# Heads transposed a tile later, averages paired, the last tile's banks in another order: one change to the front of an encoder layer

## The chip, the cores and the metric

One core of a Trainium2 chip runs the whole program. The metric is the time of one execution on the device, in microseconds (us); with several runs, their median. The core has four engines that compute: TensorE (PE; its weight load is listed as PEld), VectorE (DVE), ScalarE (ACT) and GpSimd (POOL). SyncE (SP) issues most of the DMA transfers, POOL a few. The engines run side by side, each its own instructions in a fixed order, and wait for each other by semaphores. TensorE writes into PSUM banks; ACT and DVE take the results from there.

## What is computed

One layer of an encoder over 2048 tokens of width 1024: attention of 8 heads with forget gates beside a pooling over trailing windows of 2, 4, 8 and 16 frames, then cross attention to 256 memory tokens, then SwiGLU. Cut to what the change touches:

```python
def rmsnorm(x, g):
    return x * lax.rsqrt(jnp.mean(x * x, axis=-1, keepdims=True) + EPS) * g
...
xn = rmsnorm(h, g_mix[l])
z = jnp.einsum('bsd,dc->bsc', xn, w_in[l])          # q, k, v, p_in, f_logit side by side
q = rmsnorm(head_split(q, FOX_HEADS, FOX_HEAD_DIM), g_q_fox[l]).transpose(0, 2, 1, 3)
k = rmsnorm(head_split(k, FOX_HEADS, FOX_HEAD_DIM), g_k_fox[l]).transpose(0, 2, 1, 3)
c = jnp.cumsum(jax.nn.log_sigmoid(f_logit), axis=-1)
s = q @ k * scale + c[t] - c[s]; causal softmax; fox = p @ v
mixed = trailing mean of p_in over POOL_WINDOWS[g] frames - p_in, group g of 4
pool = (mixed @ w_pool[g]) * pool_scale
h = h + concat(fox, pool) @ w_out[l]
mn = rmsnorm(mem, g_mem_kv[l]); mkv = mn @ w_mem_kv[l]   # 256 memory tokens
...
h = h + cross attention of h to mkv (4 heads)
h = h + SwiGLU(rmsnorm(h, g_ffn[l]))
```

All matmuls of the projections are made in three products (high by high, low by high, high by low parts of float32), so each "matmul" below stands for three instructions.

## The kernel before

**Stage A** (0 to about 102 us) computes the 512 pooling columns, transposed, in eight blocks of 256 tokens, while the weights of the other 1544 columns arrive and are split (`split_w_in`). For the norms it needs sums of squares of each token row: `load_rows(i)` fetches the 128 tokens of tile i (two loads), `square_rows(i)` squares them on ACT with a running sum, and `row_stats(T)` turns four tiles' sums into the factors `rstd` and stores them.

**The tile loop** (about 102 to 416 us) runs over 16 tiles of 128 tokens, i = 2b + j. `project(i, j, hs, ls, banks)` makes 1544 columns in four PSUM banks of 386, 24 matmuls each; there are four such buffers, so bank n of a tile can start when bank n of the tile before has been copied out. `scaled` does that on ACT, times `rstd`, into a slab z. `normed_heads` then splits v into high and low parts and stores it, adds the gates' bias, and takes the squares of q and k with their sums (DVE) and their inverse roots (POOL). One tile later `split_heads` multiplies q and k by these and by the gains (DVE), and splits the result: a cast on ACT, the low part on DVE (`kl`, L55). `to_heads` transposes it: 16 transposes on PE in four groups q = 0 to 3 (L410), each copied to a stage buffer `st` by ACT (L412) and stored by SP (L413) in `qkT`. Before, groups 0 to 2 stand at the end of the tile in which `split_heads` was run, right behind that tile's last bank, and group 3 behind bank 0 of the next.

In the same loop run the 16 pooled averages, w = 4T + g for token quarter T and window group g. `window_load` fetches the columns; `window` (DVE) multiplies by `rstd` (rows `rb`), makes g + 1 additions of shifted columns (L204), subtracts the frame (L459) and splits (L199 on ACT, L55 on DVE); `pooled` (PE) applies the group's map in the single PSUM bank `ss`, and its second half copies it out (ACT, L478) and stores it in `poolT` (POOL, L479). Before, one average stands in each of tiles 0 to 5 and 8 to 13, and two in tiles 6 and 7. The loop also prepares the output weights (`out_sums`) in eight of the tiles.

These steps take their buffers from 14 job slots `jl`. A freed slot goes to the end of a list and the next request takes the first of the list, so the order of frees in the program decides which earlier use a new one waits for, its store included. `in_order` fixes the order of DVE, ACT, POOL and SP as the program has it.

**The memory stage** (about 416 to 460 us) makes the keys and values of the memory, `kv(0)` to `kv(15)`, each six matmuls in three products of a weight block that `split_kv(n)` has split (ACT L194, DVE L195). Among them stand tile 15's `split_heads` and `to_heads`, the matmuls of the memory's squares `ssp`, and `cumulated`, which makes the running sum of the gates in steps, one at each `next(cum)`: two DVE steps (L519, L520), log and exponent on ACT (L521, L522, with a table load), a difference on DVE (L524), totals by a matmul with ones (L527), sums inside the blocks by a triangular matrix (L533), a transpose (L537), a store in `cd`. SP issues the 16 weight loads `kr`, then head 0's queries and keys of the first three token quarters (15 loads), then the last four stores. Then **head 0** starts (scores `sps`, L799), and the rest of the program follows to 2594 us.

Of the kernel before, what the change touches and what calls it, by code (L numbers as in the profile page):

```python
# [8 lines left out]
F32 = mybir.dt.float32  # L9
# [7 lines left out]
P = 128  # L17
# [23 lines left out]
def block_kernel(ctx: ExitStack, tc: tile.TileContext, x, xT, memT, cols, rows, w_qkvf, w_p, w_pool, w_out,  # L41
# [128 lines left out]
    def x_split(tiles, part=None, qs=range(4)):  # L170

        for q in qs:
            n, raw = tiles[q]
            hi = xp.tile([P, 2, B], F32R, tag="xhi", name="xhi", bufs=8)
            act.copy(hi[:], raw[:])
            if part is not None:
                sq = part.v if q == 0 else zp.tile([P, 4, P], F32, tag="st", name="sq", bufs=4)[:].rearrange("p a c -> p (a c)")
                act.activation(sq.rearrange("p (a t) -> p a t", a=2), raw[:], AF.Square, scale=1.0 / 32.0)
                if q:
                    pool.tensor_tensor(out=part.v, in0=part.v, in1=sq, op=ALU.add)  # L180
# [54 lines left out]
    head0, zs_home = [], hpa  # L235
    with xstack, in_order(EN.DVE, EN.Activation, EN.Pool, EN.SP):
        was = ExitStack()
        wa = opened(was, "wa", side="right")
# [49 lines left out]
        msx = small([P, NT], "msx")  # L288
        rows_in = {}

        def load_rows(i):
# [46 lines left out]
        for b in range(1, NB):  # L338
            hs, ls = x_parts(xt)
            nxt_raw = x_load((b + 1) % NB)  # L340
            load_w_in(b)
            for s_ in stores:
                s_()
            zs = [zpp.tile([P, 2, B], F32, tag="z", name="zp", bufs=4) for _ in range(2)]
            load_rows(b - 1)
# [5 lines left out]
            square_rows(b - 1)  # L351
# [16 lines left out]
        def scaled(i, zps):  # L368
            z = slab(i % 2)
            for n in zps:  # L370
                act.activation(z[:, n * ZB:(n + 1) * ZB], zps[n][:], AF.Copy, scale=rstd[:, i:i + 1])
            return z

        def normed_heads(i, z):

            vq = slab(3)
# [4 lines left out]
            sp.dma_start(vd[:, :, i, :].rearrange("h p c -> p h c"), vq[:, :1024].rearrange("p (h c) -> p h c", h=H))  # L381
            dve.tensor_tensor(out=fl[:, :, i], in0=z[:, 1536:1544], in1=bfor, op=ALU.add)

            qn = vq[:, 1024:]
# [3 lines left out]
            dve.tensor_reduce(out=ms[:], in_=qf, axis=AX.X, op=ALU.add)  # L388
            rq = small([P, 2 * H], "zrq", 2)
            rsqrt(rq[:], ms[:])  # L390
            return z, qn, rq

# [11 lines left out]

        def to_heads(i, zr, qs):
            for q in qs:
# [5 lines left out]
                act.copy(st[:], tp[:])  # L412
                sp.dma_start(qkT[q][i // 4][:, :, i % 4 * P:(i % 4 + 1) * P].rearrange("h p t -> p h t"), st[:])  # L413

# [92 lines left out]
        def cumulated():  # L507
# [17 lines left out]
            yield  # L525
            tot = one_bank()
            pe.matmul(tot[:, :HN], lhsT=ones[:], rhs=e, start=True, stop=True)  # L527
# [4 lines left out]
            loc = one_bank()  # L532
            pe.matmul(loc[:, :HN], lhsT=utri, rhs=e, start=True, stop=True)  # L533
            dve.tensor_tensor(out=e, in0=loc[:, :HN], in1=cp[4], op=ALU.add)
# [4 lines left out]
            sp.dma_start(cd[:], mn)  # L539
            yield  # L540

        kvraw, kvw, kvb = {}, {}, {}
        EARLY = 8

# [28 lines left out]
        xt = nxt_raw  # L573
        zr, st_, mxs, jobs = None, None, [], {}
# [3 lines left out]
        pts = {0: window_load(0, 0)}  # L578
        for b in range(NB):
            hs, ls = x_parts(xt)  # L580
            for j in range(2):
                i = 2 * b + j
                if j == 0:
# [3 lines left out]
                if i < 9:  # L587
                    load_rows(i + 7)
                if i >= 12:
                    for n in {14: range(3), 15: range(3, EARLY)}.get(i, ()):  # L590
                        load_kv(n)
                elif i in sums_at:
                    jobs["sums"] = out_sums_load(sums_at.index(i))
# [14 lines left out]
                if i < 9:  # L608
                    square_rows(i + 7)
                if i > 0:  # L610
                    zr = split_heads(*st_)
                if i == NT - 1:
                    split_kv(0)
                    split_kv(1)
                if "sums" in jobs:
                    out_sums(sums_at.index(i), jobs.pop("sums"))
                if i in (0, 4, 8):
                    row_stats((i + 7) // 4)
                if i == NT - 1:
                    was.close()  # L620
                    kvp = opened(xstack, "kvp", side="right")
# [11 lines left out]
        here[0] = kvp  # L633
        jobs_in[0] = Slots(kvp, [P, TB + HIS], "kl", 6)
        kv(0)
        split_kv(2)
        split_kv(3)
        kv(1)
# [5 lines left out]
        mms, mr = small([P, 2], "mms"), small([P, 2], "mr")  # L644
        dve.tensor_copy(mms[:], ssp[:, :2])
        rsqrt(mr[:], mms[:])
        st_ = normed_heads(NT - 1, z)
        for n in range(4, EARLY):
            split_kv(n)
# [6 lines left out]
        cum = cumulated()  # L656
        next(cum)
        next(cum)
        kv(2)
        kv(3)  # L660
        split_kv(8)
        next(cum)
        kv(4)
        zr = split_heads(*st_)
        next(cum)
        kv(5)
        split_kv(9)
        kv(6)
        split_kv(10)
        kv(7)  # L670
        to_heads(NT - 1, zr, range(4))
        next(cum)
        kv(8)
# [4 lines left out]
        for m in range(2):  # L678
            act.activation(msk[m].v, mks[m].v, AF.Square)
        next(cum)  # L680
        load_gates(0, head0[3])
        load_head_part(0, head0, 3)
# [1086 lines left out]
```

## Time and profile before

| | us |
|---|---|
| median of 3 runs | 2598.14 |
| lowest and highest | 2594.37, 2600.2 |
| the profiled execution, its own time | 2595.92 |
| its span in the profile | 2594.1 |
| mean granted TensorE clock | 0.989 |

The profile is one execution. A row of a timeline or a group tells the line of the kernel (L410), the operation, what is written from what, and in brackets how long the engine stood idle before it and what released it. Tile starts in this execution (first matmul of bank 0): tile 1 at 118.57, tile 4 at 176.35, tile 7 at 238.35, tile 8 at 261.74, tile 15 at 397.46; the memory stage starts at 416.47 and head 0 at 460.45.

### The profile page before, as it was taken

To read this page: it belongs to the slowest core of one execution; us is meant where nothing else is said; L and a number is where in the kernel's file an instruction comes from. 1 tells how busy PE (TensorE), PEld (TensorE's weight loads), DVE (VectorE), ACT (ScalarE), POOL (GpSimd) and SP (SyncE) were. 2 spreads that over 40 slices of the span, in tenths; PEclk is the share of its full clock that TensorE was granted. 3 is DMA by queue.
4 is the path that set the end of the run, shared out by engine and by line. 5 is a ranking of instruction groups with operands and counts; after the bars stand their busy time and mean duration, and the time that the engine had idled before them with its cause. 6 is when DMAs were issued, how large, how long until landed. Compare 5 with 4: busy or idle time off the path is not lost.

```text
span 2594.1 us, 37306 instructions
## 1 busy us (share of the span) xinstructions
PE 2519.7 (97%) x12909; PEld 2161.3 (83%) x12909; DVE 1733.9 (67%) x2995; ACT 1297.4 (50%) x2487; POOL 829.0 (32%) x1134
## 2 busy tenths in 40 slices
PE   8999998999999799999999999999999999999998
PEld 8998997788888587788878888888888888888887
DVE  4466564899998755455787778756766666665554
ACT  5455445788889413555643433334543333333443
POOL 0132333445555522344425445431001222222000
PEclk9999998999999999999999999999999999999999
DMA  8775657744542646222554554447773332325765
GB/s 260 218 219 163 186 161 199 208 123 122 150 123 61 191 157 203 89 82 90 179 207 171 195 183 169 168 158 261 244 266 130 104 119 102 122 102 177 233 211 187
DMA packets 248558, 434.01 MB, mean 167 GB/s; under 512 B 30000, under 2 KB 121904, under 8 KB 240688
## 3 DMA queue, kind: packets, MB, share of 16 engines
q1 hardware_dynamic: 215216, 323.59, 39.7%
q0 software_dynamic: 33152, 108.03, 11.4%
q8 instruction: 102, 1.67, 0.3%
q14 instruction: 88, 0.72, 0.1%
HBM read 294.02 MB, written 137.50 MB: 166 GB/s over the span
## 4 chain that ended last, share of the span: by engine, by line
PE 48%; issue 8%; DVE 2%; ACT 1%; DMA 1%; POOL 1%; SPq 0%; POOLq 0%; DVEq 0%; ACTq 0%
PE bk L62 13%; PE bk L60 13%; PE bk L61 13%; PE mmps L60 2%; PE mmps L62 2%; PE mmps L61 2%; PE tp L980 1%; PE obk L60 0%; DVE ww L55 0%; DMA xraw<-hTd 0%; PE obk L62 0%; PE obk L61 0%; POOL out_dram L1662 0%; DMA h<-h1d 0%; ACT mq L1153 0%
## 5 line engine op out<-in xcount | busy, mean ns | idle before, releaser
L55 DVE TENSOR_TENSOR ww<-draw,ww 128x512 fp32r<-128x512 f32 x308 | 204.9, 702 | 156.2 <-ACT ww L199 155.7
L199 ACT CAST ww<-draw 128x512 fp32r<-128x512 f32 x308 | 179.1, 620 | 220.5 <-PE bk L62 175.7
L55 DVE TENSOR_TENSOR ww<-graw,ww 128x512 fp32r<-128x512 f32 x220 | 180.9, 829 | 104.4 <-ACT ww L199 104.0
L61 PE MATMUL bk<-ww,ww 128*128 128x512 f32 x616 | 239.8, 389 | 0.0
L62 PE MATMUL bk<-ww,ww 128*128 128x512 f32 x616 | 239.8, 389 | 0.0
L60 PE MATMUL bk<-ww,ww 128*128 128x512 f32 x616 | 239.8, 389 | 0.0
L199 ACT CAST ww<-graw 128x512 fp32r<-128x512 f32 x220 | 135.8, 621 | 181.8 <-PE bk L62 158.6
L55 DVE TENSOR_TENSOR pl<-tp,ph 128x512 fp32r<-128x512 f32 (+3 forms) x296 | 176.7, 598 | 33.4 <-ACT ph L893 31.6
L812 ACT ACTIVATE s<-s,mx 128x1024 f32<-128x1024 f32 (+2 forms) x192 | 173.7, 905 | 6.0 <-DVE mx L806 5.4
L60 PE MATMUL zps<-wh,xhi 128*128 128x386 f32 x512 | 175.2, 342 | 0.0
L877 PE MATMUL tp<-ident,s 128*128 128x128 f32 x1088 | 172.4, 274 | 2.3 <-DVE pl L55 1.8
L61 PE MATMUL zps<-wl,xhi 128*128 128x386 f32 x512 | 174.1, 340 | 0.0
L62 PE MATMUL zps<-wh,xl 128*128 128x386 f32 x512 | 173.6, 339 | 0.0
L893 ACT CAST ph<-tp 128x512 fp32r<-128x512 f32 (+3 forms) x296 | 148.6, 513 | 41.0 <-PE tp L877 34.7
L877 PEld LDWEIGHTS tp<-ident,s 128*128 128x128 f32 x1088 | 134.5, 142 | 30.9 <-DVE pl L55 5.7
L1662 POOL DMA_DIRECT2D out_dram<-o x32 | 17.3, 540 | 382.6 <-DVE o L1659 381.6
L62 PE MATMUL bk<-qs,ww 128*128 128x512 f32 x352 | 137.3, 390 | 1.4 <-DVE ww L55 1.4
L60 PE MATMUL bk<-qs,ww 128*128 128x512 f32 x352 | 137.9, 392 | 0.3 <-ACT s L1581 0.3
L61 PE MATMUL bk<-kh,ww 128*128 128x512 f32 x352 | 137.0, 389 | 0.0
L60 PE MATMUL bk<-kl,ww 128*128 128x512 f32 x352 | 137.0, 389 | 0.0
L62 PE MATMUL bk<-kl,ww 128*128 128x512 f32 x352 | 137.0, 389 | 0.0
L61 PE MATMUL bk<-cb,ww 128*128 128x512 f32 x352 | 137.0, 389 | 0.0
(608 smaller groups left out, 7275.7 us busy)
## 6 DMA issues: line engine op xcount, KB each, us to landing
graw<-in_w_gu_dram SPq DMA_DIRECT2D x44, 1024.0 KB, 5.4
draw<-in_w_down_dram SPq DMA_DIRECT2D x66, 256.0 KB, 4.4
xl<-in_xT_dram SPq DMA_DIRECT2D x64, 256.0 KB, 4.7
wdr<-in_w_down_dram SPq DMA_DIRECT2D x22, 512.0 KB, 4.6
jl<-in_x_dram SPq DMA_DIRECT2D x32, 256.0 KB, 6.6
vd<-cb SPq DMA_DIRECT2D x16, 512.0 KB, 4.6
cb<-cd SPq DMA_DIRECT2D x8, 1024.0 KB, 7.4
v<-vd SPq DMA_DIRECT2D x8, 1024.0 KB, 5.4
```

The lines of the kernel that those rows point to most:

```text
L55: (eng or dve).tensor_tensor(out=lo, in0=src, in1=f(hi), op=ALU.subtract)
L60: pe.matmul(ps, lhsT=sh, rhs=mh, start=first, stop=False, skip_group_check=goes_on)
L61: pe.matmul(ps, lhsT=sh, rhs=ml, start=False, stop=False, skip_group_check=goes_on)
L62: pe.matmul(ps, lhsT=sl, rhs=mh, start=False, stop=last, skip_group_check=goes_on)
L199: act.copy(hi, raw)
L812: act.activation(s[:, sl], s[:, sl], AF.Exp, bias=ng, scale=-1.0, accum_out=l[:, q, g:g + 1])
L877: pe.transpose(tp[:, q * P:(q + 1) * P], unit["rows"][q][:, j * P:(j + 1) * P], ident[:])
L893: act.copy(ph[:, sl], tp[:, sl])
L980: pe.transpose(tp[:, e_], src[:, q + e_], ident[:])
L1662: pool.dma_start(out[rows_, cs], o)
```

## The change

- `to_heads(i - 2, ...)` now does all four groups in tile i: groups 0 and 1 behind bank 0, groups 2 and 3 behind bank 1. Nothing is transposed at the end of a tile, except tile 13's heads, at the end of tile 14.
- The averages stand in tiles 0 to 11: the short windows (g = 0 and 1) as a pair in tiles 0, 3, 6 and 9, the others one by one.
- Stage A squares ten row groups (before seven), the loop the other six. The output weights are prepared in other tiles.
- The memory's sums of squares are added on DVE (before POOL).
- The last tile makes its banks in the order 3, 2, 1, 0, each copied out at once. `cumulated` stands between them, with the two matmuls of the totals in one bank. The first two weight blocks are split in it. `normed_heads` is cut in `split_v`, `gates` and `norms`.
- Six weight loads are early (before eight), eight come before head 0's loads, two behind them and behind the load of the gates. The memory stage has four job slots of another size and four stage buffers (before six and three).
- The last four stores of heads go out on POOL's queue.

The diff, cut:

```diff
@@ x_split
-                    pool.tensor_tensor(out=part.v, in0=part.v, in1=sq, op=ALU.add)
+                    dve.tensor_tensor(out=part.v, in0=part.v, in1=sq, op=ALU.add)
...
-        stage = lambda name: here[0].tile([P, 4, P], F32, tag="st", name=name, bufs=4 if here[0] is zp else 3)
+        stage = lambda name: here[0].tile([P, 4, P], F32, tag="st", name=name, bufs=4)
...
+        ROWS = (0,), (1, 2), (3, 4), (5, 6), (7,), (8,), (9,)
...
-        row_stats(0)
+        for T in range(2):
+            row_stats(T)
...
-        def to_heads(i, zr, qs):
+        def to_heads(i, zr, qs, queue=sp):
...
-                sp.dma_start(qkT[q][i // 4][:, :, i % 4 * P:(i % 4 + 1) * P].rearrange("h p t -> p h t"), st[:])
+                queue.dma_start(qkT[q][i // 4][:, :, i % 4 * P:(i % 4 + 1) * P].rearrange("h p t -> p h t"), st[:])
...
-            tot = one_bank()
-            pe.matmul(tot[:, :HN], lhsT=ones[:], rhs=e, start=True, stop=True)
-            dve.tensor_copy(cp[3], tot[:, :HN])
+            both = one_bank()
+            tot, loc = both[:, :HN], both[:, HN:2 * HN]
+            pe.matmul(tot, lhsT=ones[:], rhs=e, start=True, stop=True)
+            pe.matmul(loc, lhsT=utri, rhs=e, start=True, stop=True)
+            dve.tensor_copy(cp[3], tot)
...
-        EARLY = 8
+        EARLY = 6
...
-        sums_at = (0, 1, 2, 3, 4, 9, 10, 11)
-        averages = lambda i: [i] if i < 6 else [2 * i - 6, 2 * i - 5] if i < 8 else [i + 2] if i < 14 else []
+        sums_at = (1, 2, 4, 5, 7, 8, 10, 11)
+        AVERAGES = (0, 1), (2,), (3,), (4, 5), (6,), (7,), (8, 9), (10,), (11,), (12, 13), (14,), (15,)
...
-                    to_heads(i - 2, zr, (3,))
+                    to_heads(i - 2, zr, range(2))
...
                     zps.update(project(i, j, hs, ls, range(n, n + 1)))
+                    if n == 1 and i > 1:
+                        to_heads(i - 2, zr, range(2, 4))
...
                 z = scaled(i, zps)
-                if i > 0:
-                    to_heads(i - 1, zr, range(3 if i < NT - 1 else 4))
-                if i < NT - 1:
-                    st_ = normed_heads(i, z)
+                if i == LAST - 1:
+                    to_heads(i - 1, zr, range(4))
+                st_ = normed_heads(i, z)
...
+        next(cum)
+        zps = project(i, 1, hs, ls, (3,))
         ssp = one_bank()
...
+        zr = split_heads(*st_)
+        scaled(i, zps)
...
+        gates(i, z)
         dve.tensor_copy(mms[:], ssp[:, :2])
         rsqrt(mr[:], mms[:])
+        next(cum)
+        zps = project(i, 1, hs, ls, (2,))
+        next(cum)
+        next(cum)
+        scaled(i, zps)
...
+        split_v(i, z, vq)
+        zps = project(i, 1, hs, ls, (1,))
+        to_heads(i - 1, zr, range(4))
+        scaled(i, zps)
...
+        split_kv(0)
+        split_kv(1)
+        zps = project(i, 1, hs, ls, (0,))
+        next(cum)
+        next(cum)
+        scaled(i, zps)
...
+        jobs_in[0] = Slots(kvp, [P, TB], "kl", 4)
         kv(0)
         split_kv(2)
+        st_, rest = norms(z, vq)
         split_kv(3)
+        rest()
         kv(1)
...
-        for n in range(EARLY, 2 * KD):
+        for n in range(EARLY, EARLY + 8):
             load_kv(n)
         head0.extend(load_head(0, hpa, range(3)))
+        load_gates(0, head0[3])
         kv(2)
         kv(3)
+        split_kv(6)
+        kv(4)
+        split_kv(7)
+        for n in range(EARLY + 8, 2 * KD):
+            load_kv(n)
+        zr = split_heads(*st_)
+        kv(5)
...
-        to_heads(NT - 1, zr, range(4))
+        to_heads(LAST, zr, range(4), pool)
```

How the order changes is shown at three places. In the rows, a wait on DMASW is one for a transfer that POOL issued, DMAHW for one of SP's, and the numbers behind a name tell buffers apart.

ACT in tile 4, from a copy of transposed heads (`st`) over the first average's way out of `ss` to the scaled copies of the tile's banks (`zps`). Before:

```order
L412 COPY st<-tp 128x512 [waits DMAHW3_49,PE_49]
L199 CAST jl_2348<-jl_2009 128x512 [waits DVE_49,PE_49]
L478 ACTIVATE jl_2266<-ss,colt 128x512 [waits DMAHW2_49,DMASW3_49,DMAHW6_49,DMASW2_49,DMASW1_49]
L298 ACTIVATE jl_2220,msx_210<-jl_2220 128x512 [waits DMAHW5_49]
L298 ACTIVATE jl_2221,msx_210<-jl_2221 128x512 [waits DMAHW6_49,DMASW6_49]
L401 CAST kl<-cb 128x16x64 [waits DVE_49,Activation_49]
L371 ACTIVATE qs<-zps,rstd 128x386 [waits Pool_49]
L371 ACTIVATE qs<-zps,rstd 128x386 [waits PE_49] x3
```

After (line numbers are those of the changed kernel: L430 is the copy of heads, L496 the average's, L419 the cast of split_heads, L376 the scaled copy):

```order
L430 COPY st<-tp 128x512 [waits DMAHW5_49,PE_49]
L430 COPY st<-tp 128x512 [waits DMAHW6_49,PE_49]
L430 COPY st<-tp 128x512 [waits DMAHW7_49,PE_49]
L430 COPY st<-tp 128x512 [waits DMAHW0_49,PE_49]
L496 ACTIVATE jl_2282<-ss,colt 128x512
L199 CAST jl_2391<-jl_2028 128x512 [waits DMASW4_49,DVE_49,Activation_49]
L496 ACTIVATE jl_2330<-ss,colt 128x512 [waits DMASW7_49,PE_49]
L300 ACTIVATE jl_2228,msx_213<-jl_2228 128x512 [waits DMAHW7_49]
L300 ACTIVATE jl_2229,msx_213<-jl_2229 128x512 [waits DMAHW0_49]
L419 CAST kl<-cb 128x16x64 [waits DVE_49]
L376 ACTIVATE qs<-zps,rstd 128x386 [waits Pool_49]
L376 ACTIVATE qs<-zps,rstd 128x386
```

All four copies of heads now stand ahead of the first average's copy, and a second average's copy behind it; the scaled copies still come last.

DVE in the same tile, the average (L204 multiplies by `rb` and then adds, L459 or L477 is its last step) and the two products of split_heads behind it. Before:

```order
L204 TENSOR_TENSOR jl_2009<-jl_2009,jl_2007 128x512 [waits DMAHW6_49,DMAHW5_49]
L442 COPY jl_2009<-tail_1402 128x16
L444 COPY tail_1402<-jl_2009 128x16 [waits DVE_49]
L204 TENSOR_TENSOR jl_2345<-jl_2009 128x527 [waits DMASW7_49]
L459 SCALAR_TENSOR_TENSOR jl_2009<-jl_2345,jl_2009 128x512 [waits DVE_49]
L55 TENSOR_TENSOR jl_2349<-jl_2009,jl_2348 128x512 [waits Activation_49]
L396 TENSOR_TENSOR cb<-kh,zrq 128x1024 [waits Pool_49]
L398 TENSOR_TENSOR cb<-cb,gqs 128x1024 [waits DVE_49]
L55 TENSOR_TENSOR kl<-cb,kl 128x16x64 [waits Activation_49]
```

After:

```order
L204 TENSOR_TENSOR jl_2028<-jl_2028,jl_1807 128x512 [waits DMAHW2_49]
L460 COPY jl_2028<-tail_1429 128x16
L462 COPY tail_1429<-jl_2028 128x16 [waits DVE_49]
L204 TENSOR_TENSOR jl_2384<-jl_2028 128x527 [waits DMASW2_49,DMASW1_49,DMASW4_49,PE_49,Activation_49]
L204 TENSOR_TENSOR jl_2386<-jl_2384 128x525 [waits DVE_49,PE_49]
L204 TENSOR_TENSOR jl_2388<-jl_2386 128x521 [waits DVE_49]
L477 SCALAR_TENSOR_TENSOR jl_2028<-jl_2388,jl_2028 128x512 [waits DVE_49]
L55 TENSOR_TENSOR jl_2392<-jl_2028,jl_2391 128x512 [waits Activation_49]
L414 TENSOR_TENSOR cb<-kh,zrq 128x1024 [waits Pool_49]
L416 TENSOR_TENSOR cb<-cb,gqs 128x1024 [waits DVE_49]
L55 TENSOR_TENSOR kl<-cb,kl 128x16x64 [waits Activation_49]
```

A window of three additions (w = 6) has taken the place of a window of one (w = 4). Its first addition writes slot `jl_2384`, and waits for DMASW4, which is POOL's store of `jl_2282`, the first average's result in the rows of ACT above.

SP at the end of the memory stage, head 0's loads (`qs`, `kh`, `kl`), the stores of tile 15's heads and of the gates (`cd`), and the gates' load (`cb`). Before:

```order
L219 DMA kh<-qkT2t_94 64x512
L220 DMA kl<-qkT2t_94 64x512
L413 DMA qkT0t_87<-st 128x4x128
L413 DMA qkT1t_91<-st 128x4x128
L413 DMA qkT2t_95<-st 128x4x128
L219 DMA kh<-qkT2t_92 64x512
L413 DMA qkT3t_99<-st 128x4x128
L539 DMA cd<-kl_4678 128x128
L220 DMA kl<-qkT2t_92 64x512
```

After:

```order
L219 DMA kh<-qkT2t_94 64x512
L220 DMA kl<-qkT2t_94 64x512
L223 DMA cb<-cd 128x2048
L569 DMA kr<-in_w_mem_kv_dram 128x512 x2
L216 DMA qs<-qkT0t_87 128x512
L219 DMA kh<-qkT2t_95 64x512
```

The four stores have left SP. The load of the gates has come ahead, and behind it stand the last two weight blocks of the memory, which before were issued ahead of all of head 0's loads.

More of the change, by code (lines that the diff above doesn't have):

```diff
@@ L236, in block_kernel @@
     with xstack, in_order(EN.DVE, EN.Activation, EN.Pool, EN.SP):
+        msmall = opened(xstack, "msmall", side="right")
         was = ExitStack()
@@ L344, in block_kernel @@
             zs = [zpp.tile([P, 2, B], F32, tag="z", name="zp", bufs=4) for _ in range(2)]
-            load_rows(b - 1)
+            for r in ROWS[b - 1]:
+                load_rows(r)
             project_p(hs, ls, zs, range(KD), (0, 1))
@@ L350, in block_kernel @@
             project_p(hs, ls, zs, range(KD), (2, 3))
-            square_rows(b - 1)
+            for r in ROWS[b - 1]:
+                square_rows(r)
             stores.append(keep_p(b, zs, 1))
@@ L381, in normed_heads, with gates, norms @@
             sp.dma_start(vd[:, :, i, :].rearrange("h p c -> p h c"), vq[:, :1024].rearrange("p (h c) -> p h c", h=H))
+        def gates(i, z):
             dve.tensor_tensor(out=fl[:, :, i], in0=z[:, 1536:1544], in1=bfor, op=ALU.add)
+        def norms(z, vq):
             qn = vq[:, 1024:]
@@ L531, in cumulated @@
             yield
-            loc = one_bank()
-            pe.matmul(loc[:, :HN], lhsT=utri, rhs=e, start=True, stop=True)
-            dve.tensor_tensor(out=e, in0=loc[:, :HN], in1=cp[4], op=ALU.add)
+            dve.tensor_tensor(out=e, in0=loc, in1=cp[4], op=ALU.add)
             yield
@@ L586, in block_kernel @@
                     pts[w] = window_load(w % NG, w // NG)
[L587 to L590, printed above, removed]
+                if i < 6:
+                    load_rows(i + 10)
+                if i in sums_at:
+                    jobs["sums"] = out_sums_load(sums_at.index(i))
+                if i >= LAST - 2:
+                    for n in range(3 * (i - LAST + 2), 3 * (i - LAST + 3)):
                         load_kv(n)
-                elif i in sums_at:
-                    jobs["sums"] = out_sums_load(sums_at.index(i))
                 zps = project(i, j, hs, ls, range(1))
                 if i > 1:
-                    to_heads(i - 2, zr, (3,))
+                    to_heads(i - 2, zr, range(2))
                 pos = []
@@ L643, in block_kernel @@
                           stop=c == 1)
-        mms, mr = small([P, 2], "mms"), small([P, 2], "mr")
+        mms, mr = (msmall.tile([P, 2], F32, name=n) for n in ("mms", "mr"))
+        zr = split_heads(*st_)
+        scaled(i, zps)
+        zt[i] = z
+        gates(i, z)
         dve.tensor_copy(mms[:], ssp[:, :2])
         rsqrt(mr[:], mms[:])
-        st_ = normed_heads(NT - 1, z)
-        for n in range(4, EARLY):
-            split_kv(n)
+        next(cum)
[3 more added lines that the diff above has]
+        scaled(i, zps)
+        zt[i] = z
+        split_v(i, z, vq)
+        zps = project(i, 1, hs, ls, (1,))
+        to_heads(i - 1, zr, range(4))
+        scaled(i, zps)
+        zt[i] = z
+        split_kv(0)
[3 more added lines that the diff above has]
+        next(cum)
+        was.close()
+        kvp = opened(xstack, "kvp", side="right")
+        scaled(i, zps)
+        here[0] = kvp
+        jobs_in[0] = Slots(kvp, [P, TB], "kl", 4)
+        kv(0)
+        split_kv(2)
+        st_, rest = norms(z, vq)
+        split_kv(3)
+        rest()
+        kv(1)
+        split_kv(4)
+        split_kv(5)
         lstack.close()
```

67 lines of the change are left out of this document (30 added, 37 removed).

## The prediction

> **What bounds the kernel now.** The page comes first, for the busy shares. Its first part gives each engine's busy time and its share of the span.
>
> ```profile
> span 2594.1 us, 37306 instructions
> PE 2519.7 (97%) x12909; PEld 2161.3 (83%) x12909; DVE 1733.9 (67%) x2995; ACT 1297.4 (50%) x2487; POOL 829.0 (32%) x1134
> ```
>
> TensorE (PE) is busy in 97% of the span, and the change takes no matmul away. All it can gain is time in which PE stands still, or runs at a lowered clock. The second view is the busy time by stretches. I cut it where the loops change: tiles 1 to 5, tiles 6 to 8, tiles 9 to 15, the memory stage (keys and values of the memory), and the start of head 0. The columns are stretch, length, busy time of each engine, granted clock, share of the DMA engines, GB/s.
>
> ```profile
> 130.00:210.00 80.00, 78.76 (x474) 77.17 (x474) 55.31 (x87) 40.84 (x77) 30.33 (x32) 1.00 0.70 206
> 210.00:290.00 80.00, 73.40 (x425) 71.27 (x424) 46.89 (x68) 41.86 (x78) 21.03 (x16) 0.96 0.57 170
> 290.00:416.00 126.00, 125.92 (x766) 124.51 (x764) 76.31 (x101) 59.38 (x102) 41.34 (x34) 1.00 0.57 168
> 416.00:461.00 45.00, 33.25 (x142) 26.14 (x143) 20.91 (x34) 21.23 (x36) 16.57 (x30) 0.81 0.91 245
> 461.00:500.00 39.00, 34.25 (x173) 26.23 (x172) 32.98 (x112) 30.02 (x65) 17.75 (x39) 0.91 0.58 175
> ```
>
> PE loses something at tiles 1 to 8 and much in the memory stage; between 290 and 416 it loses nothing. The third view, the waits of PE from 116 to 500, says what ended the idle time: total, times, longest.
>
> ```profile
> PE tp L410 <- DVE kl L55: 7.8, 7, 2.3
> PE kv L60 <- ACT kw L194: 7.0, 1, 7.0
> PE ss L527 <- DVE kl L524: 4.6, 1, 4.6
> PE sps L799 <- DVE mx L801: 4.2, 4, 2.4
> ```
>
> The first three are what the change touches. The fourth belongs to head 0, whose code stays.
>
> **What the stalls cost, clock included.** PE's timeline after the stall at the end of tile 6:
>
> ```profile
> 236.86 1.69 PE L410 MATMUL tp<-identr,kl 128*128 128x128 f32 x12 [2.29 <-DVE kl L55]
> 239.44 0.53 PE L60 MATMUL zps<-wh,xhi 128*128 128x386 f32 x1
> 240.38 0.34 PE L60 MATMUL zps<-wh,xhi 128*128 128x386 f32 x1
> ```
>
> After 2.29 us of idleness matmuls take 0.53 instead of 0.34 us until 240.4. Against the even pitch of the tile this stretch lost about 1.0 us more than the wait; two of the seven stalls are that long, and the five shorter ones have no such stretch. Wait, issue gaps and slow clock together make **11.3 us** for the seven (7.8 waited, 2.1 of clock, 1.4 of gaps).
>
> In the memory stage, PE's timeline:
>
> ```profile
> 429.20 0.76 PE L527 MATMUL ss<-kl,ones 128*128 128x128 f32 x2 [4.63 <-DVE kl L524]
> 431.04 0.63 PE L60 MATMUL kv<-kw,xhi 128*128 128x512 f32 x1
> 434.88 0.41 PE L60 MATMUL kv<-kw,xhi 128*128 128x512 f32 x1
> 440.45 0.40 PE L60 MATMUL kv<-kw,xhi 128*128 128x512 f32 x1
> 441.15 0.40 PE L60 MATMUL kv<-kw,xhi 128*128 128x512 f32 x1
> 449.74 0.79 PE L60 MATMUL kv<-kw,xhi 128*128 128x512 f32 x1 [7.02 <-ACT kw L194]
> ```
>
> Three matmuls take 0.70 us at 440.45 and 1.28 us at 431.04 (three groups to 434.88). So the wait for the gates, 4.63, cost 2.5 more by the clock, and the wait of 7.02 another 2.9. With 0.9 of small gaps about it the stage loses **18 us**. ACT and SP tell where the 7.02 came from:
>
> ```profile
> 436.79 1.56 ACT L412 COPY st<-tp 128x512 f32<-128x512 f32 x3 [3.02 <-PE tp L410]
> 446.29 0.58 ACT L412 COPY st<-tp 128x512 f32<-128x512 f32 x1 [7.94 <-DMA qkT0t<-st]
> ```
>
> ```profile
> 421.56 4.61 SPq L549 DMA_DIRECT2D kr<-in_w_mem_kv_dram  x8
> 441.13 0.45 SPq L220 DMA_DIRECT2D kl<-qkT2t  x1
> 441.86 0.38 SPq L413 DMA_DIRECT2D qkT0t<-st  x1
> ```
>
> The fourth copy waited for one of three stage buffers; the store that frees it stood in SP's order behind head 0's loads. The weight split that PE needed stood behind this copy on ACT.
>
> **Part 1: heads transposed a tile later.** Transposes and copies stay 16 and 4 a tile. They now read a tile that was split one tile before, so the wait at the tile's end has no cause left: **-11.3**. Late next is the new tile's bank 0, which needs the first scaled copy. That copy stands on ACT behind the cast of split_heads, which stands behind DVE's averages.
>
> **Part 2: pairs of short averages.** The averages' number is the same; the double long ones of tiles 6 and 7 go apart. Rows of tile 0, whose single average becomes two, DVE then ACT:
>
> ```profile
> 110.42 1.08 DVE L204 TENSOR_TENSOR jl<-jl,jl 128x512 f32<-128x512 f32 x1 [3.08 <-DMA jl<-pd]
> 111.63 0.70 DVE L204 TENSOR_TENSOR jl<-jl 128x527 f32<-128x527 f32 x1
> 112.78 0.69 DVE L459 SCALAR_TENSOR_TENSOR jl<-jl,jl 128x512 f32<-128x512 f32 x1
> 114.42 0.69 DVE L55 TENSOR_TENSOR jl<-jl,jl 128x512 fp32r<-128x512 f32 x1 [0.74 <-ACT jl L199]
> ```
>
> ```profile
> 113.77 0.62 ACT L199 CAST jl<-jl 128x512 fp32r<-128x512 f32 x1 [7.15 <-DVE jl L462]
> 114.72 0.63 ACT L298 ACTIVATE jl<-jl 128x512 f32<-128x512 f32 x1 [0.33 <-DMA jl<-in_x_dram]
> 116.04 1.51 ACT L371 ACTIVATE qs<-zps,rstd 128x386 f32<-128x386 f32 x3
> ```
>
> The first average ends on DVE at 115.1. The second adds 1.08, two additions of 0.70, the last step 0.69 and about 0.8 of small copies, so its cast on ACT begins at 119.1; then cast 0.62, two squares 1.32, one scaled copy 0.5: 121.6. PE was to begin tile 1 at 118.6: **+3.0**, and **+1.1** of clock (a wait like the 2.29).
>
> In tiles 4, 7 and 10 PE applies two averages over one PSUM bank. The second waits until ACT has copied the first out, and that copy now stands behind the copies of heads 2 and 3. Rows by group of lines, mean ns after the comma:
>
> ```profile
> L412 ACT COPY st<-tp 128x512 f32<-128x512 f32 x58 | 31.2, 592 | 18.7 <-PE tp L410 18.4
> L401 ACT CAST kl<-cb 128x1024 fp32r<-128x1024 f32 x15 | 15.7, 1046 | 29.6 <-DVE cb L398 29.6
> L478 ACT ACTIVATE jl<-ss,colt 128x512 f32<-128x512 f32 x16 | 11.0, 684 | 0.6 <-PE ss L62 0.6
> ```
>
> From the end of the transposes: about 0.15 until the last copy begins, 0.59 for it, 0.68 for the average: 1.4 each, **+4.2**. It would be nothing if bank 2 stood between; it doesn't.
>
> The same tiles, and tile 1, bring a wait that the diff does not show: the next long average takes a slot that the first average's result has just left, so DVE waits until POOL's store of it has landed. How long that takes is in the view of the tile poolT:
>
> ```profile
> DMA to landing us min/median/max: 2.3/5.9/7.5
> ```
>
> Tile 4, from the start T of its bank 0 (bank 4.38, eight transposes 1.13, first average 0.7): ACT has copied the first average at T+12.9. Landing at 2.3 to 7.5 gives T+15.2 to T+20.4. DVE then needs three additions (2.2), last step and split (2.1 with ACT's cast between), the two products of split_heads (2.4), and ACT the cast of 1.05: 7.9. The first scaled copy ends 0.6 later, at T+23.7 to T+28.9, while PE is through with the tile at T+22.5: a stall of 1.2 to 6.4. I take 2.5 and 1.0 of clock, because at T+13 most of the tile's loads are in. By the same working tiles 1 and 7 give 0.6 each and tile 10 2.1. Together **+6.8** (bounds 1.5 to 17). Short hold-ups behind three more tiles where a pair meets the split of x: **+1.3** (0 to 2).
>
> The tile loop comes out at -11.3 + 4.1 + 4.2 + 6.8 + 1.3 = **+5.1**. Stage A squares ten row groups instead of seven, three times two squares on ACT at 0.8. It has room, by the busy times from 50 to 102:
>
> ```profile
> 50.00:102.00 52.00, 52.00 (x434) 52.00 (x434) 19.46 (x23) 26.68 (x50) 1.48 (x3) 1.00 0.76 247
> ```
>
> PE never stands still there and ACT is idle for 25 us, so these 4.8 us lie beside PE's work: nothing, up to +2 if their 1.5 MB of loads delay weights.
>
> **Part 3: the last tile.** What goes: the 4.63 and 7.02 with their clock, **-18.0** with the gaps. What comes, T0 being PE's end of tile 14:
>
> ```profile
> 403.86 0.69 DVE L55 TENSOR_TENSOR xl<-xl,xhi 128x512 fp32r<-128x512 f32 x1 [0.24 <-ACT xhi L175]
> 405.62 5.77 POOL L180 TENSOR_TENSOR jl<-jl,sq 128x512 f32<-128x512 f32 x3
> ```
>
> - The sums of squares of the memory are matmuls behind bank 3, at T0+5.9 (sixteen transposes 1.67, a bank 4.2). Before, T0 was 396.65 and DVE ended the splits at T0+7.9; three additions, now DVE's at about 0.7 and partly in gaps, end at T0+9.5. Stall 3.7, clock 1.8: **+5.5** (2 to 8).
> - The gates' totals between banks 2 and 1: 0 to the 4.63 of now; bank 2 gives 4.2 of cover. **+1.5**.
> - The last transposes still stand behind norms, split_heads: 2.4 and 1.0 of clock, **+3.4** (0 to 5). One weight split late: **+0.9**.
> - Weights 14 and 15 are now issued behind 15 loads of head 0 and the gates' load. By SP's rows 23 loads took 421.6 to 441.6, so their issue comes at about 443.5 and the landing some 6 later; PE wants them, split, at about 451: **+2.3** (0 to 4.7).
>
> Sum -18.0 + 13.6 = **-4.4**. The last stores no longer wait behind loads; head 0 needs them no sooner than its other loads: nothing.
>
> **Sum.** +5.1 - 4.4 = +0.7 on the profiled execution's 2595.92, 2596.6. That execution lies 2.2 below the median of the runs shown, 2598.14, so in those terms **2598.8**.
>
> **A rule against a row.** The Trainium skill ("TensorE: Matmul & The Clock Gate", part 1, the HAM clock gate) says that the clock falls to half after an idle window of about 3.4 us. By that rule the new stalls under 3.4 us cost no clock, and the sum would be lower by 3.1. The trace disagrees: 2.29 us was enough; I keep the row's price.
>
> **Rivals.**
> - *Landings in time* (20%): the stores land in 2.3 us, weights 14 and 15 arrive early, the squares come without loss of clock: 6.8 + 2.3 + 1.8 less, **2588**. For it: the loads of tile 4 are fewer at T+13 than at its start. Against: the median landing is 5.9.
> - *Only the removed waits count* (10%): 29.3 less and only tile 0's 4.1 added, **2573**. Against it: in tiles 4, 7 and 10 ACT's order alone gives the 1.4.
> - *The slot decides* (20%; the slower side): in tiles 4, 7 and 10 the store lands after 6 to 7.5 us. DVE is late, ACT's cast and the scaled copy behind it, and PE stands at bank 0 of tiles 5, 8 and 11; each adds about 3, with clock, to what I took: **2608**. It decides where the landing takes more than some 4 us.
> - *The wait only changes its name* (8%): DVE's lateness at the ends of tiles 5 to 8 stays and PE waits for the scaled copy in place of the transposes. Half of the 11.3 comes back, less the 1.3 counted: **2603**.
>
> **How the numbers follow.** My forecast has 42%, own range 2593 to 2603. About 0.2%, 5.2 us, is what a measurement of this kernel can tell from no change. Faster: the first two rivals, 0.30. Slower: the third, half the fourth and the upper tail, 0.25. Same: 0.45. The range leaves out the 2573 case and the outer tails: 2584 to 2611.
>
> **What would show it.** Right: no wait of the transposes for kl behind tiles 4 to 8; new waits of the projection for the scaled copy at tiles 1 and 5; of the pooled matmul for ACT in tiles 4, 7, 10; one of the sums of squares for DVE; none for the kw split near 442. Wrong: PE busy through 116 to 416 (then near 2588), or waits of 4 us and more at tiles 5, 8, 11 (then near 2608), or head 0 starting much later than 456 to 460.

## The result and the profile after

The changed kernel is slower: 2621.19 us, the median of 4 runs (2617.75 to 2622.01), against 2596.36 (2594.37 to 2600.2) for the kernel before (4 runs, the three above and one more). The ratio is 1.0091 with a 95% interval of 1.0074 to 1.0109. The profiled execution took 2621.78 against 2595.92.

The first part of the page after, and its waits of PE in the first 520 us, which take in the start of head 0 (engine, line, releaser, total, times, longest). Lines have moved: the copy of heads is L430, the scaled copy L376, the average's way out L496, the score matmul of head 0 L848.

```profile
span 2619.9 us, 37306 instructions
PE 2525.7 (96%) x12909; PEld 2165.7 (83%) x12909; DVE 1733.3 (66%) x2998; ACT 1298.8 (50%) x2487; POOL 820.5 (31%) x1135
```

```profile
PE zps L60 <- ACT qs L376: 12.8, 5, 4.0
PE zps L60 <- ACT kh L376: 8.0, 4, 2.4
...
PE sps L848 <- DVE mx L850: 4.9, 4, 3.1
PE ss L60 <- ACT jl L496: 4.3, 3, 1.4
PE ss L664 <- POOL jl L532: 3.4, 1, 3.4
PE tp L428 <- DVE kl L55: 2.7, 1, 2.7
PE kv L60 <- ACT kw L194: 1.4, 1, 1.4
```

Every wait that the change meant to remove is gone or small: the seven of the transposes in the loop, the 7.02 of the weights' split (1.4 now), the 4.63 of the gates. In their place PE waits nine times for a scaled copy, 20.8 us in all. Before, it did so at no place of the loop. The busy times by stretch, cut as in the prediction, show where: PE stood still for 5.8, 9.8 and 6.1 us, before for 1.2, 6.6 and 0.1. So the loss is spread over the loop, also over its later tiles, which lost nothing before.

```profile
130.00:210.00 80.00, 74.22 (x425) 71.84 (x423) 45.28 (x75) 32.65 (x61) 21.20 (x24) 0.98 0.59 179
210.00:290.00 80.00, 70.17 (x409) 68.43 (x409) 53.77 (x82) 36.50 (x66) 28.37 (x28) 0.98 0.55 165
290.00:416.00 126.00, 119.91 (x724) 118.00 (x723) 67.63 (x90) 56.43 (x95) 32.59 (x30) 1.00 0.56 169
```

**Tile 4 to 5, step by step.** DVE after, in time order:

```profile
190.69 1.07 DVE L204 TENSOR_TENSOR jl<-jl,jl 128x512 f32<-128x512 f32 x1
205.35 2.26 DVE L204 TENSOR_TENSOR jl<-jl 128x527 f32<-128x527 f32 x3 [13.29 <-DMA poolT<-jl]
209.68 1.22 DVE L414 TENSOR_TENSOR cb<-kh,zrq 128x1024 f32<-128x1024 f32 x1
```

ACT and PE over the same stretch:

```profile
198.58 1.07 ACT L430 COPY st<-tp 128x512 f32<-128x512 f32 x2 [4.56 <-PE tp L428]
199.54 0.70 ACT L496 ACTIVATE jl<-ss,colt 128x512 f32<-128x512 f32 x1
212.19 1.04 ACT L419 CAST kl<-cb 128x1024 fp32r<-128x1024 f32 x1 [1.35 <-DVE cb L416]
213.14 2.00 ACT L376 ACTIVATE qs<-zps,rstd 128x386 f32<-128x386 f32 x4
```

```profile
213.77 0.57 PE L60 MATMUL zps<-wh,xhi 128*128 128x386 f32 x1 [4.04 <-ACT qs L376]
```

ACT stood idle for 4.56 us, because its next instruction in order was the copy of the heads' group 2, which PE transposes only behind bank 1. Then came the first average's copy, at 199.5. Its store was issued at 200.53 and landed some 4.8 us later, and that freed the slot for which DVE had waited 13.29 us. The rest is the chain of the prediction: additions, split_heads, cast, scaled copy, PE.

**Tile 3 to 4** shows the same order with another victim. ACT, then DVE, then PE at the start of tile 4:

```profile
175.42 1.07 ACT L430 COPY st<-tp 128x512 f32<-128x512 f32 x2 [4.48 <-PE tp L428]
176.38 0.64 ACT L199 CAST jl<-jl 128x512 fp32r<-128x512 f32 x1
```

```profile
177.04 0.69 DVE L55 TENSOR_TENSOR jl<-jl,jl 128x512 fp32r<-128x512 f32 x1 [2.29 <-ACT jl L199]
```

```profile
186.55 0.65 PE L60 MATMUL zps<-wh,xhi 128*128 128x386 f32 x1 [2.30 <-ACT kh L376]
```

The pair's first average was ready on DVE at 174.8. Its cast stood behind the copies of heads, so DVE lost 2.29 us in the middle of a pair. PE waited 2.30 us for the scaled copy at tile 4's start, and with the slow matmuls behind this wait it lost 4.1. At the pair of tile 6 DVE waited 5.71 us for the same cast, at that of tile 9 2.90.

Head 0 starts at 479.81 against 460.45, 19.4 us later. The other 5 us of the 24.8 between the medians come behind that point.

### The profile page after: what moved, and what is told of

The parts are those of the page before. It is cut to its first block, busy times and chain, and to the rows that moved or that the text cites. A ratio compares the mean times of both kernels' runs of the same rounds, so it can differ in the third digit from the quotient of the medians.

```text
span 2619.9 us, 37306 instructions
## 1 busy us (share of the span) xinstructions
PE 2525.7 (96%) x12909; PEld 2165.7 (83%) x12909; DVE 1733.3 (66%) x2998; ACT 1298.8 (50%) x2487; POOL 820.5 (31%) x1135
## 4 chain that ended last, share of the span: by engine, by line
PE 47%; issue 8%; DVE 2%; ACT 1%; DMA 1%; POOL 1%; SPq 0%; POOLq 0%; DVEq 0%; ACTq 0%
PE bk L62 13%; PE bk L60 13%; PE bk L61 13%; PE mmps L62 2%; PE mmps L60 2%; PE mmps L61 2%; PE tp L1029 1%; DMA xraw<-hTd 0%; DVE ww L55 0%; POOL out_dram L1711 0%; DMA h<-h1d 0%; DMA wqr<-in_w_mem_q_dram 0%; ACT mq L1202 0%; DVE ms L1206 0%; DMA hTd<-hst 0%
## 5 line engine op out<-in xcount | busy, mean ns | idle before, releaser
L60 PE MATMUL zps<-wh,xhi 128*128 128x386 f32 x512 | 179.3, 350 | 20.8 <-ACT qs L376 12.8
L55 DVE TENSOR_TENSOR pl<-tp,ph 128x512 fp32r<-128x512 f32 (+3 forms) x296 | 177.0, 599 | 33.5 <-ACT ph L942 31.9
```

What stands on the lines that cost most here:

```text
L55: (eng or dve).tensor_tensor(out=lo, in0=src, in1=f(hi), op=ALU.subtract)
L60: pe.matmul(ps, lhsT=sh, rhs=mh, start=first, stop=False, skip_group_check=goes_on)
```

## The experiments

Each was timed beside the kernel before, whose medians there were 2596.4 to 2598.4; the ratio is to that. "Head 0" is the start of its first score matmul in the run's profile, which is one execution.

| run | median us | ratio, 95% interval | head 0 |
|---|---|---|---|
| before | 2596.4 | | 460.5 |
| changed kernel | 2621.2 | 1.0074 to 1.0109 | 479.8 |
| changed, averages of before | 2605.4 | 1.0015 to 1.0044 | 468.4 |
| before, heads a tile later | 2597.8 | 0.9993 to 1.0015 | 462.1 |
| only the end changed | 2601.1 | 1.0005 to 1.0028 | 457.4 |
| changed, own buffers | 2607.6 | 1.0023 to 1.0049 | 467.5 |
| changed, four groups at once | 2606.9 | 1.0026 to 1.0052 | 464.5 |
| before, heads later, four at once | 2593.0 | 0.9975 to 0.9998 | 458.8 |
| changed, own buffers and four at once | 2594.6 | 0.9976 to 0.9997 | 456.5 |
| the same, pairs in even tiles | 2588.2 | 0.9958 to 0.9982 | 450.6 |
| the same, end reordered | 2590.8 | 0.9964 to 0.9982 | 451.2 |
| that loop with the old end | 2588.8 | 0.9954 to 0.9980 | 451.3 |
| the same, stores on POOL | 2589.3 | 0.9950 to 0.9980 | 450.5 |

**Averages of before in the changed kernel.**

```diff
-        averages = lambda i: AVERAGES[i] if i < len(AVERAGES) else ()
+        averages = lambda i: [i] if i < 6 else [2 * i - 6, 2 * i - 5] if i < 8 else [i + 2] if i < 14 else []
```

> The changed kernel with the averages of the kernel before: one in each of tiles 0 to 5 and 8 to 13, two long ones in tiles 6 and 7. Theory A (the pairs of short averages and the slots they leave make the loss; transposing heads a tile later gains): the loop is rid of the waits at tiles 1, 4, 5, 7, 8, 10, 11 (33 us in the changed kernel) but for some 3 to 8 us, head 0 starts at 449 to 456 us, total 2586 to 2597. Theory B (the heads' copies, now all four ahead of the averages on ACT, make it, whatever the averages): most of the waits stay, total above 2605.

Between the theories: the total of 2605.4 just meets B's mark, but head 0 at 468.4 and the waits (11.3 us for scaled copies, 20.8 in the changed kernel) lie between. All tiles with one average are free of waits. Around the two with two long averages PE lost 3.9, 5.7 and 2.2 us and some clock behind them. So the averages' places carry 11 of the 19.4 us up to head 0, but heads a tile later still hurt wherever two averages meet.

**Only the heads a tile later.**

```diff
-                    to_heads(i - 2, zr, (3,))
+                    to_heads(i - 2, zr, range(2))
...
+                    if n == 1 and i > 1:
+                        to_heads(i - 2, zr, range(2, 4))
...
-                if i > 0:
-                    to_heads(i - 1, zr, range(3 if i < NT - 1 else 4))
+                if i == NT - 1:
+                    to_heads(i - 1, zr, range(4))
```

> The kernel before with only the heads transposed a tile later. Theory A: the 11.3 us of stalls behind kl go and 0 to 6 come back as waits for the scaled copy, total 2585 to 2592. Theory B: as many or more waits for the scaled copy or for the averages' copy come, total 2596 or above.

2597.8, no change, in theory B's range, where theory A wanted 2585 to 2592. The 11.3 us are gone and came back in tiles 6 and 7. ACT and DVE of this run in tile 6:

```profile
222.99 1.07 ACT L412 COPY st<-tp 128x512 f32<-128x512 f32 x2 [4.54 <-PE tp L410]
223.95 0.63 ACT L199 CAST jl<-jl 128x512 fp32r<-128x512 f32 x1
```

```profile
219.95 0.69 DVE L459 SCALAR_TENSOR_TENSOR jl<-jl,jl 128x512 f32<-128x512 f32 x1
224.61 0.69 DVE L55 TENSOR_TENSOR jl<-jl,jl 128x512 fp32r<-128x512 f32 x1 [3.97 <-ACT jl L199]
```

The average was ready at 220.6 and its cast came at 223.95. Theory A falls in this form. A third theory took its place: ACT's order, in which casts and copies of averages stand behind copies of heads that wait for PE, works together with pairs of averages and their slots.

**Only the end changed.** Averages and transposes of the loop as before, the rest as changed:

```diff
-                    to_heads(i - 2, zr, range(2))
+                    to_heads(i - 2, zr, (3,))
...
-                if i == LAST - 1:
-                    to_heads(i - 1, zr, range(4))
+                if i > 0:
+                    to_heads(i - 1, zr, range(3 if i < LAST - 1 else 4))
```

> The changed kernel with the tile loop's averages and transposes as before, so that of the change the last tile, the memory stage, the ten early row squares and the places of the output weights are left. Theory A (the end gains 3 us up to head 0): head 0 starts at 456 to 458 us. On the 5 us that the changed kernel lost behind head 0's start: if they come from the new end (loads of head 0, gates, stores), the total is 2596 to 2600; if they were a matter of the one execution, 2592 to 2595.

Head 0 at 457.4, 3.0 earlier, as expected; total 2601.1, 4.4 above before and 1.1 above even the range for a cost of the new end. The wait for the squares of the memory, which has taken the place of the one for the gates, is released by the addition that was moved to DVE:

```profile
408.00 1.29 PE L661 MATMUL ss<-ones,jl 128*128 128x1 f32 x8 [3.41 <-DVE jl L180]
```

So the end gains up to head 0, and in this run more than that was lost behind it.

**Own buffers for the averages' results.**

```diff
-            po = Slot()
+            po = small([P, TB], "po", 2)
...
```

> The changed kernel with two buffers of their own for the averages' results in place of job slots. If DVE's waits for the landing of poolT are what holds tiles 5, 8 and 11 (5.8, 2.5 and 2.7 us) and 2 (1.4): 7 to 12 us less, 2609 to 2614, and PE waits at tiles 4, 7 and 10 (the pairs) stay. If DVE and ACT would be late there anyway: 0 to 3 us less.

2607.6, 13.6 us less than the changed kernel and more than the 7 to 12 expected. DVE's waits for additions in the changed kernel, then in this run:

```profile
DVE jl L204 <- DMA poolT<-jl: 35.4, 4, 13.3
```

```profile
DVE jl L204 <- PE ss L62: 11.3, 5, 5.8
```

Four waits of 35.4 us for stores became five of 11.3 for slots that PE still reads, and in tile 4 DVE takes the average's last step 5.7 us sooner behind the tile's start. PE's waits for the scaled copy behind tiles 1, 4, 7 and 10 are gone. The waits at tiles 4, 7 and 10 for the first average's copy stay, as expected.

**Four groups at once.** In the changed kernel all four groups of heads behind bank 0:

```diff
-                    to_heads(i - 2, zr, range(2))
+                    to_heads(i - 2, zr, range(4))
...
-                    if n == 1 and i > 1:
-                        to_heads(i - 2, zr, range(2, 4))
```

> The changed kernel with all four groups of heads transposed behind bank 0, so that on ACT no copy of heads waits for bank 1. Theory C (ACT's order is the cause: the casts and copies of the averages stand behind copies of heads that wait for PE): the waits at tiles 4, 7 and 10 for the first average's copy (1.7 each) and at the ends of tiles 3, 6 and 9 (2.4 each, one with 1.7 of clock) go, the slot waits of tiles 4, 7 and 10 shorten by 1 to 4 each, the fourth group may cost 0.3 a tile: 2602 to 2611. Theory D (DVE's work for two averages is too long for a tile whatever ACT's order): only the 1.7 each go, 2613 to 2619.

2606.9, in theory C's range. In tile 3 ACT is done with the copies of heads before the average is ready:

```profile
169.40 2.05 ACT L430 COPY st<-tp 128x512 f32<-128x512 f32 x4 [0.29 <-PE tp L428]
173.94 0.62 ACT L199 CAST jl<-jl 128x512 fp32r<-128x512 f32 x1 [2.48 <-DVE jl L477]
```

The waits at the ends of tiles 3, 6 and 9 and those at tiles 4, 7 and 10 for the copy are gone. What stays is tile 0 and the slots. In tile 4 DVE still waits 10.25 us:

```profile
199.86 2.25 DVE L204 TENSOR_TENSOR jl<-jl 128x527 f32<-128x527 f32 x3 [10.25 <-DMA poolT<-jl]
```

The store is issued 8.4 us behind the tile's start there, 14.0 in the changed kernel, but lands after 7.4 us instead of some 4.8. From 190 to 200 us of that profile the DMA engines were busy all the time. So of the 5.6 us that the earlier copy gained, DVE got 3.0. PE was through with the tile 3 us sooner too, so its wait behind tile 4 stayed at 4.0.

**The same in the kernel before**, with heads a tile later and nothing else:

> The kernel before with the heads transposed a tile later, all four groups behind bank 0. Theory C: of the 16 us of waits that the split form had around tiles 6 and 7 at most 6 are left, 0 to 4 us for the fourth group, head 0 starts at 450 to 456 us, total 2586 to 2593. Theory D: those waits stay but for the 1.7 each, total 2594 to 2600.

2593.0, at the edge of theory C's range. Around tiles 6 and 7 PE still loses some 6 us. Head 0 came at 458.8, later than expected, because the old end lost a further 3.5, clock included, where, in the last tile, the fourth group of tile 13's heads waited for ACT's copies, which stood behind the split of the memory.

**Both in the changed kernel.**

> The changed kernel with both: own buffers for the averages' results and all four groups behind bank 0. Theory C with the slots as second cause: of the loop's waits only tile 0's 5 us and less than 3 us at tiles 3, 6 and 9 are left, head 0 starts at 452 to 458 us, total 2592 to 2600. Theory D: 2603 to 2606.

2594.6. The four runs of changed, own buffers, four at once, and both are 2621.2, 2607.6, 2606.9 and 2594.6: the two causes nearly add up, 13.6 and 14.3 alone, 26.6 together. What is left in the loop is tile 0 and 0.8 us behind tile 3:

```profile
PE sps L845 <- DVE mx L847: 3.9, 4, 2.0
PE ss L661 <- POOL jl L531: 3.4, 1, 3.4
PE zps L60 <- ACT qs L376: 3.3, 1, 3.3
PE tp L428 <- DVE kl L55: 2.8, 1, 2.8
PE kv L60 <- ACT kw L194: 1.8, 1, 1.8
```

**Pairs in even tiles.**

```diff
-        sums_at = (1, 2, 4, 5, 7, 8, 10, 11)
-        AVERAGES = (0, 1), (2,), (3,), (4, 5), (6,), (7,), (8, 9), (10,), (11,), (12, 13), (14,), (15,)
+        sums_at = (1, 2, 4, 5, 7, 9, 10, 11)
+        AVERAGES = (0,), (1,), (2,), (3,), (4,), (5,), (6,), (7,), (8, 9), (10,), (11,), (12,), (13, 14), (15,)
```

> As the run with own buffers and four groups at once, with the averages one a tile but for two pairs, in tiles 8 and 12 (w = 8, 9 and 13, 14), where DVE has no split of x at the tile's start, and the output weights' step of tile 8 in tile 9. Tile 0's 5 us go; if the loop is then rid of all waits, head 0 starts at 446 to 452 us and the total is 2586 to 2594, below both kernels.

2588.2, below both kernels. The loop has no wait of PE left; what remains is the end and head 0:

```profile
PE sps L845 <- DVE mx L847: 4.2, 4, 2.4
PE ss L661 <- POOL jl L531: 3.4, 1, 3.4
PE tp L428 <- DVE kl L55: 2.8, 1, 2.8
PE kv L60 <- ACT kw L194: 2.5, 1, 2.5
PE ss L545 <- DVE jl L541: 1.6, 1, 1.6
```

**The end reordered.**

```diff
+        zps = project(i, 1, hs, ls, (2,))
         ssp = one_bank()
...
-        to_heads(LAST, zr, range(4), pool)
         split_kv(10)
         kv(8)
+        to_heads(LAST, zr, range(4), pool)
```

> As the run with even pairs, and in the end two steps moved: the matmuls of the memory's squares go behind bank 2 instead of bank 3, tile 15's transposes behind kv(8) instead of kv(7). If PE waits at these two places for what DVE has just not finished (3.6 and 1.5 of clock; 2.9 and 1.8 of clock), 5 us go at the first and 2 to 3 at the second, head 0 starts at 442 to 445 us, and the total is 2579 to 2586. If the wait only moves on to the next step (the gates' totals, the first scaled copy of tile 15, later weights), head 0 starts at 447 to 451 us and the total stays at 2586 to 2591.

The wait only moved on: head 0 at 451.2. The matmuls of the squares and the transposes wait no more, and the gates' totals wait in their place:

```profile
PE ss L545 <- DVE jl L541: 7.0, 1, 7.0
PE kv L60 <- ACT kw L194: 4.0, 3, 2.0
```

**That loop with the old end.** The kernel before with four groups at once, own buffers and the even pairs.

> The kernel before (its end too) with the loop of the run with even pairs: heads a tile later, four groups behind bank 0, own buffers, pairs in tiles 8 and 12. The old end takes 3 us longer up to head 0 than the new one by the runs so far: head 0 starts at 450 to 456 us. If the new end costs some 5 us behind head 0's start, the total is 2584 to 2589, not above that of the even pairs with the new end; if what differs there is chance, the total is 2590 to 2594.

Head 0 at 451.3, total 2588.8: beside a loop without waits the old end is as good as the new one, within 1 us (its loop was 1.3 us shorter, its end 1.7 longer). The total lies in the range set for a cost of the new end behind head 0, but it is no lower than with the new end (2588.2), and its five runs spread from 2583.9 to 2592.8. So it doesn't decide that question.

**Only the stores on POOL's queue**, added to that run:

```diff
-        to_heads(NT - 1, zr, range(4))
+        to_heads(NT - 1, zr, range(4), pool)
```

> As the run with the old end, and only the last four stores of heads on POOL's queue, still with three stage buffers. If the store's landing (4.0 us in that run) is what the fourth copy waits for, and SP's order only 1 to 2 us of it: the copy's wait falls from 4.5 to 2.5 to 3.5 us, PE's wait for the weights' split (3.7, and 3.0 of clock) by 1 to 2, head 0 starts at 448 to 451 us, total 2585 to 2589. If the order behind SP's loads held it (landing 2.3 once issued from POOL): PE's wait goes, head 0 starts at 444 to 447 us, total 2581 to 2585.

2589.3 and head 0 at 450.5. The fourth copy's wait fell from 4.50 to 4.47: POOL issued the first store 2.7 us behind the start of the three copies ahead, SP 1.9, and it landed after 3.2 us instead of 4.0. PE's wait for the weights' split, in the run with the stores on SP and then in this one:

```profile
PE kv L60 <- ACT kw L194: 3.7, 1, 3.7
```

```profile
PE kv L60 <- ACT kw L194: 3.5, 1, 3.5
```

The queue alone is worth nothing here, less than either reading had it. That leaves the fourth stage buffer and the moved steps for what the change gained there; no run tells these two apart.

## Why the prediction was wrong

The forecast was 2598.8 in a range to 2611; it came out at 2621. The step that failed is part 2: its terms came to 33.5 us where 16.4 were put down, above all because copies of heads that wait for PE hold up the averages' casts on ACT, which no term priced. The working, by its own terms:

- **Part 1, -11.3: right, but its cover was misread.** No transpose in the loop waits for kl any more, and with the averages of before nothing came back in tiles with one average. The prediction costed the moved transposes as PE's own and named the scaled copy as next late. It did not count the four copies on ACT as a place in ACT's order: with two of them behind bank 1, ACT stands idle for 4.5 us in the middle of a tile, and what stands behind them of the averages is late. The run with the heads alone shows it (no gain), the runs with four groups at once show it undone, in the changed kernel wholly, in the kernel before but for some 6 us.
- **Part 2, +16.4: the step that failed.** The figures are PE's lost time at each place, against its even pitch (some 0.2 us more than the wait that the profile gives). The largest miss is "short hold-ups behind three more tiles, 1.3 (0 to 2)": they were 9.7, far over the bound, 0.9 behind tile 2, 4.1 behind tile 3, 2.4 behind tile 6, 2.3 behind tile 9. The prediction had no term for a pair whose own cast waits behind the copies of heads. The slot waits cost 12.4 (6.8, bounds to 17): 1.4 behind tile 1, 5.8 behind tile 4, 2.5 behind tile 7, 2.7 behind tile 10. Here the mechanism was right and the choice within the bounds was bad: in the prediction's count from T, the start of tile 4's bank 0, a stall of 2.5 needs a landing some 3.6 us behind T+12.9, while the store was issued at T+14.0 and DVE went on at T+18.8. Tile 0 cost 3.5 and 2.8 of clock (4.1 predicted), the second average in tiles 4, 7 and 10 cost 5.1 (4.2). Sum 33.5 for 16.4.
- **Part 3, -4.4: right.** From the last matmul of tile 14's banks to head 0 it took 64.1 us before and 60.3 after, -3.9. That it came so near is partly luck: in the other runs with the new end, the reordered one aside, the same stretch took 59.2 to 62.7. Its waits came as listed: squares of the memory 3.4, transposes of tile 15 2.7, weights 1.4. The first is released by DVE's moved addition in the run with only the end changed, as the prediction had it; in the changed kernel the releaser shown is POOL's L532, which ended at about the same moment.
- **"Rest unchanged": off by 5 us, and open.** The kernels with the new end lost 0.8 to 7.4 us more than before behind head 0's start (median total less the profile's head 0, against before), those with the old end -1.9 to 2.2. In the profiles most of the difference arises some 400 to 600 us and some 800 to 900 us behind head 0's start, where PE waits for DVE at the same instructions in every kernel, and more or less so from one execution to the next. Runs of the same end differ by more than 6 us. Whether the new end causes a part of it is not settled.
- **The rivals.** "The slot decides" was the right direction (20%, 2608): DVE late, the cast and the scaled copy behind it, PE at bank 0 of tiles 5, 8 and 11, where it waited 4.0, 2.4 and 2.5 us. From the issue of the store until DVE went on it took 4.6 to 4.8 us, over its mark of some 4 and under its 6 to 7.5. With own buffers all three waits go; with four groups at once that of tile 8 goes, and 4.0 and 2.2 stay. It named one of two causes. The other, of like size, was no rival.
- **The clock.** In the changed kernel waits of 2.30, 4.04 and 3.31 us by the profile were followed by 1.65, 1.64 and 2.85 us lost in slow matmuls; the granted clock was 0.50 from 124 to 126 us, behind the wait of 3.31. Waits of 1.4 were followed by none. Four others of 2.19 to 2.50 (behind tiles 6, 7, 9 and 10) had none either, with a granted clock of 1.00 behind them, and neither had the wait of 3.01 at the same place of tile 1 in the run with four groups at once. So the price taken from the row of 2.29 us was too sure: an idle time of about that length sometimes costs clock and sometimes not, and part of tile 0's 2.8 is chance. The traces bear out neither the idle window of about 3.4 us of the Trainium skill ("TensorE: Matmul & The Clock Gate", part 1, the HAM clock gate) as the least idle time that costs clock nor 2.3 us as a sure trigger.

## What to carry to other kernels

When work is moved on one engine, write down the order of every engine that handles its output, and look for an instruction there that waits for something late while other engines' work stands behind it: moving transposes on PE moved copies on ACT, and these held up a cast that DVE needed. A buffer taken from a list of freed slots inherits the last user's store as a wait, so pairing producers changes who waits for which store. Both causes went with small edits (all four transposes and copies in one place, two own buffers, 27 us together), while reordering a tuned end only moved its wait on.

## What was not expected of the hardware

In the stretch from 500 to 900 us behind head 0's start PE waited from 15.5 to 22.4 us in the profiles of kernels that differ only in their first 480 us, and the totals of one unchanged kernel ran from 2589.1 to 2604.6. Against that, kernels that share the loop took the same time for it, from the first matmul of tile 0 to the last of tile 14's banks: 286.3 us in both with the new end and even pairs, 285.0 in both with the old end. So the start of head 0 told two variants of the loop apart better than their totals did.
